# A hybrid decoder layer on one core: transposes of x and of the second norm inside projection columns, RWKV's turned keys in 2 KB runs, decayed keys of the right-hand sides turned by VectorE

## The chip, the cores and the metric

One core of one Trainium2 chip. The metric is the device time of one execution in microseconds (us), given as the median of several runs.

## The reference, cut to what matters

The input x is 1 x 2048 x 1024, in float32, as everything is. The layer runs two kinds of linear recurrence side by side, then a feed-forward block.

```python
h = _rmsnorm(x, norm1_w[l])
proj = h @ w_in[l]                                   # 3840 columns
...
o_hg = _hgrn2_mixer(...)                             # 4 heads of 128: columns q, f, i, g
o_rw = _rwkv7_mixer(...)                             # 8 heads of 64: r, k, v and three low-rank inputs
x = x + jnp.concatenate([o_hg, o_rw], axis=-1) @ w_out[l]
x = x + _conv_ffn(_rmsnorm(x, norm2_w[l]), ...)      # width 2816, causal convolution of 3
...
return _rmsnorm(x, final_norm_w)
```

RWKV's recurrence for each head, with a 64 x 64 state S, is

```python
sa = jnp.einsum('bhvk,bhk->bhv', S, at)
S = S * wt[:, :, None, :] + sa[..., None] * bt[:, :, None, :] + vt[..., None] * kt[:, :, None, :]
y = jnp.einsum('bhvk,bhk->bhv', S, rt)
```

The kernel computes it in chunks of 64 tokens: within a chunk, the vectors `sa` of all tokens solve a triangular system, whose matrix is made of products of decayed keys. Its right-hand sides hold, for each token, the decayed key `at` (what the state adds is a product with it) and what the values of the chunk's earlier tokens add.

## The kernel before, in words

**Phase 1** (to about 1250 us) does norm, projection, both recurrences and the out-projection of the first three blocks of tokens; the rest is the last block's out-projection and the feed-forward block, which the change leaves as they are. Phase 1 takes the 2048 tokens in 4 blocks of 512. Channels lie on the 128 partitions and tokens along the free axis.

`dense()` yields TensorE's large work as a list of jobs per block. The main one is a *column* ("P"): 128 columns of `w_in` times the normed x of the block, hh + hl (high and low part), over 8 slices k of 128 channels, three products of 128 x 512 each (`mm3`, L270 to L272), so 24 wide matmuls into one bank of PSUM. Two banks called `pj` are used in turn. The column's eviction (`ev_rkv`, `ev_q` and so on) reads the bank on ScalarE, and for most kinds on VectorE too, and only then the bank is free for the column after the next. A block has 31 columns in this order: 1 low-rank, 6 rkv, 8 of HGRN2 (q, f, v, g for two heads), 1 low-rank, 6 rkv, 8 of HGRN2. Every ScalarE operation goes through the helper `act` (L122) and every split in high and low part through L247 to L255, so these lines stand for many operations in the profile.

Other jobs are inserted between columns by their place in the list (`extra`, L543 on):
- "E" runs `load4` (four DMAs of 128 rows of the next block's x into `xt`) or `norm4` (scales each row by its norm, in place).
- "T" runs `turn` (L437): 8 groups, each of four 128 x 128 transposes on TensorE (L443) into a `pj` bank, which ScalarE copies back into `xt`. The next block's x is so turned in one go, for blocks 1, 2 and 3.
- "N" runs `transposed` (L258) for the second norm of block nb - 2: the rows come back from DRAM (`x1d`), are turned in the same manner (L264), scaled by ScalarE (`to_h2`, L490) and stored to DRAM (`h2d`) by a DMA of the SP queue (L494). It runs twice in phase 1's columns.
- "O" is the out-projection of block nb - 2.

RWKV's heads are worked in 8 *supers* (`rw_super`): one block of tokens and two pairs of heads (index u) each. HGRN2's heads are 16 units (`hg_unit`). The main loop takes one piece of each stream in turn and then as many dense pieces as a fixed credit holds, so pieces of the heads lie among the columns in the instruction queues. Engines take their queue strictly in order, and DMAs that a stream issues with `dma` stand in SP's queue in the order of the program.

A super, as far as the change touches it: VectorE makes the decayed keys `AT` (inside the tile `AR`) and `KB`. TensorE makes the products `M` (L730), VectorE masks them (L733). The triangular blocks go through DRAM into `E` (L745, L748), and VectorE inverts 32 x 32 blocks in 31 steps (L802, L804). Its result is transposed by VectorE into `TZ` (L808) and `TTs` (L814), and TensorE goes on with it at L821, L834 and L847. Meanwhile two things are turned from channels on partitions to tokens on partitions:
- `KBT`, the turned keys: VectorE transposes 32 x 32 squares of `KB` into `KBb` (L754), and 16 DMAs on SP move the squares to their partitions (L757), in runs of 128 bytes. TensorE reads `KBT` at L867 as weights (64 channels of one chunk and head per matmul, neighbours in memory) and in half of L881 as moving data.
- `RHS`, the right-hand sides: TensorE transposes `AT` (8 transposes per super, L765) into PSUM and two ScalarE copies (L774, L775, seen as L122) put it in `RHS`. The other half of `RHS` comes from L782 on. L847 reads it.

Of the kernel before, what the change touches and what calls it, by code (L numbers as in the profile page):

```python
# [67 lines left out]
def tile_layer(ctx, tc, consts, x, norm1_w, w_in, hg_lb_logits, hg_norm_w, rw_shift_mu, rw_w0, rw_w2,  # L68
# [205 lines left out]
    def phase1(c1):  # L274
# [162 lines left out]
        def turn(nb):  # L437

            t_ = rows[nb]
            for k in range(KD):  # L440
                tp = bank("pj")
                for i in range(4):
                    TE.transpose(tp[:, i * P:(i + 1) * P], t_[:, i, k * P:(k + 1) * P], ident)  # L443
                act(t_[:, :, k * P:(k + 1) * P], tp.rearrange("p (i t) -> p i t", i=4), AF.Copy)
                yield 436
# [43 lines left out]

        def to_h2(nb):  # L490
            def evict(k, tp, w):
                t_ = wp.tile([P, BLK], F32, tag="wraw", name="h2", bufs=4)
                act(t_, tp, AF.Copy, scale=w)
                dma(h2d[nb][k * P:(k + 1) * P, :], t_)  # L494
            return evict
# [20 lines left out]
        def dense():  # L516
# [63 lines left out]
            ahead = iter(())  # L580
            for n, jb in enumerate(jobs):
# [8 lines left out]
                if jb[0] == "T":  # L590
                    yield from turn(jb[1])
                    continue
                if jb[0] == "N":
                    yield from transposed(four_tiles(rows.pop(jb)), "n2", lambda: bank("pj"), to_h2(jb[1]))
                    continue
# [51 lines left out]
        def rw_super(nb, s_):  # L647
# [102 lines left out]
            KBT = tile_("KBT", [2, 8, P], "KBT")  # L750
            KBb = tile_("UV", [16, 4, 32], "KBb")
            KBv = KBb.rearrange("p n a c -> p (n a) c")
            for u in U:
                V.transpose(KBv[:, 32 * u:32 * u + 32], KB[:, 4 * u:4 * u + 4].rearrange("p b k (a t) -> p (b k a) t", t=32))  # L754
            for g in range(4):
                for a in range(4):
                    dma(KBT[32 * a:32 * a + 32].rearrange("p u i t -> p (u i) t")[:, :, 32 * g:32 * g + 32],  # L757
                        KBb[32 * g:32 * g + 32, :, a, :])
# [3 lines left out]
            tp = bank2()  # L762
            for u in U:
                for b in range(4):
                    TE.transpose(tp[:, u, b * P:(b + 1) * P], AT[:, u, 2 * b:2 * b + 2, :], ident)  # L765
            tpv = tp.rearrange("p u (b h t) -> p (u b) h t", h=2, t=64)
# [7 lines left out]
            act(RHS[64:128, :, :, 0:64], tpv[0:64], AF.Copy)  # L774
            act(RHS[0:64, :, :, 0:64], tpv[64:128], AF.Copy)  # L775
# [87 lines left out]
            for u in U:  # L863
                for ch in range(8):
                    b, e = ch // 2, ch % 2
                    for h in range(2):
                        TE.matmul(xp[h * 64:h * 64 + 64, u, ch * 64:ch * 64 + 64], KBT[:, u, ch, h * 64:h * 64 + 64],  # L867
                                  UV[:, 4 * u + b, e, h * 64:h * 64 + 64], start=ch == 0, stop=False,
                                  tile_position=(0, h * 64), skip_group_check=True)
# [755 lines left out]
```

## Time and profile before

| | before |
|---|---|
| time, median of 3 runs | 2650.35 us (2645.74 to 2656.13) |
| profiled execution | 2645.42 us |
| its span | 2643.6 us |
| mean granted TensorE clock | 0.994 |
| DMA | 380298 packets, 518.98 MB, mean 196 GB/s |
| packets under 512 B | 114463 |

The span is what the profiler recorded from the first instruction to the last; the execution's own time is a little longer. In the views, "L443" is line 443 of the kernel before; "out<-in" are the tiles that an instruction writes and reads; in square brackets stands how long the engine waited ahead of the instruction, and for which engine, tile and line. A row of the waits reads: instruction that waited, what it waited for, then sum in us, number of waits and the longest. A row with a count (x512) gives shortest, middle and longest duration in ns and the first and last time in us. A row of windows gives length, then busy time of PE, PEld, DVE, ACT, POOL and SP with instruction counts, then granted clock, the DMA engines' busy share and GB/s.

### The profile page before, as it was taken

How to read it: one execution, taken by the hardware profiler on the slowest of the kernel's cores; microseconds unless marked ns; L12 is line 12 of the kernel's file. 1: busy time of each engine (PE TensorE's matmuls, PEld its weight loads, DVE VectorE, ACT ScalarE, POOL GpSimd, SP SyncE). 2: the span in 40 equal slices, each digit the busy share in tenths (PEclk: the TensorE clock that was granted, in tenths of full speed). 3: DMA queues.
4: the chain of work that ended last, by engine and by line, in shares of the span. 5: the costliest groups of instructions: out<-in, count | busy, mean ns of one | idle time of the engine just before them, and what ended most of it. 6: DMA issues, size and time to landing. Idle time of an engine off the chain costs nothing.

```text
span 2643.6 us, 51054 instructions
## 1 busy us (share of the span) xinstructions
PE 2547.0 (96%) x19467; PEld 2046.8 (77%) x19467; DVE 1963.7 (74%) x3744; ACT 1372.7 (52%) x2258; POOL 382.1 (14%) x686
## 2 busy tenths in 40 slices
PE   7999999999999999899899999999999999999998
PEld 5877777777777767777678888887888887888887
DVE  4868677676576765777678789988988887766556
ACT  5555444555545555344466654556554544545444
POOL 6433222212222122232100000000000000000000
PEclk9999999999999999999999999999999999999999
DMA  8846463555655565845583467747763553998655
GB/s 304 239 147 195 152 168 116 143 159 205 190 173 138 174 212 179 261 151 150 181 287 124 136 221 257 240 154 232 245 203 129 171 171 128 334 321 283 200 191 187
DMA packets 380298, 518.98 MB, mean 196 GB/s; under 512 B 114463, under 2 KB 211093, under 8 KB 380053
## 3 DMA queue, kind: packets, MB, share of 16 engines
q1 hardware_dynamic: 325521, 337.38, 40.1%
q0 software_dynamic: 54464, 178.32, 20.9%
q8 instruction: 153, 2.51, 0.4%
q14 instruction: 92, 0.75, 0.1%
q10 hardware_dynamic: 68, 0.02, 0.0%
HBM read 372.99 MB, written 134.22 MB: 192 GB/s over the span
## 4 chain that ended last, share of the span: by engine, by line
PE 70%; DVE 11%; ACT 8%; DMA 7%; issue 3%; POOL 0%; SPq 0%; DVEq 0%; ACTq 0%; POOLq 0%
PE pj L270 7%; PE pj L271 7%; PE pj L272 6%; PE ua L270 5%; PE ua L272 5%; PE ua L271 5%; PE da L271 3%; PE da L272 3%; PE da L270 3%; PE ud L271 2%; PE ud L270 2%; PE ud L272 2%; PE db L272 2%; PE db L271 2%; PE db L270 2%
## 5 line engine op out<-in xcount | busy, mean ns | idle before, releaser
L270 PE MATMUL pj<-hh,wh 128*128 128x512 f32 x960 | 391.6, 408 | 6.1 <-ACT rkv L122 4.0
L271 PE MATMUL pj<-hl,wh 128*128 128x512 f32 x960 | 377.4, 393 | 0.0
L272 PE MATMUL pj<-hh,wl 128*128 128x512 f32 x960 | 377.4, 393 | 0.0
L270 PE MATMUL ua<-Bh,uwh 128*128 128x512 f32 x704 | 276.4, 393 | 3.5 <-ACT m L122 2.2
L272 PE MATMUL ua<-Bh,uwl 128*128 128x512 f32 x704 | 274.3, 390 | 0.0
L271 PE MATMUL ua<-Bl,uwh 128*128 128x512 f32 x704 | 274.1, 389 | 0.0
L270 PEld LDWEIGHTS pj<-hh,wh 128*128 128x128 f32 x960 | 180.9, 189 | 54.5 <-issue 7.0
L272 PEld LDWEIGHTS pj<-hh,wl 128*128 128x128 f32 x960 | 180.8, 188 | 39.4 <-DMA wl<-Win171l 0.3
L271 PEld LDWEIGHTS pj<-hl,wh 128*128 128x128 f32 x960 | 181.0, 189 | 35.0 <-DVE hl L488 0.5
L254 ACT CAST uwh<-uraw 128x512 fp32r<-128x512 f32 x220 | 134.3, 617 | 135.0 <-PE ua L271 55.7
L255 DVE TENSOR_TENSOR dal<-draw,dah 128x512 fp32r<-128x512 f32 x138 | 95.2, 690 | 108.3 <-ACT dah L254 105.7
L255 DVE TENSOR_TENSOR uwl<-uraw,uwh 128x512 fp32r<-128x512 f32 x220 | 147.1, 684 | 34.3 <-ACT uwh L254 34.3
L254 ACT CAST dah<-draw 128x512 fp32r<-128x512 f32 x138 | 85.8, 621 | 160.0 <-PE da L271 75.5
L270 PEld LDWEIGHTS ua<-Bh,uwh 128*128 128x128 f32 x704 | 132.2, 188 | 33.9 <-ACT m L122 5.6
L272 PEld LDWEIGHTS ua<-Bh,uwl 128*128 128x128 f32 x704 | 132.2, 188 | 28.1 <-DVE uwl L255 0.4
L271 PEld LDWEIGHTS ua<-Bl,uwh 128*128 128x128 f32 x704 | 132.3, 188 | 26.7
L270 PE MATMUL ud<-Bh,uwh 128*128 128x512 f32 x352 | 138.0, 392 | 0.0
L1495 POOL DMA_DIRECT2D gd<-y x2 | 1.1, 542 | 943.1 <-DVE y L1493 943.1
L272 PE MATMUL ud<-Bh,uwl 128*128 128x512 f32 x352 | 137.1, 390 | 0.0
L271 PE MATMUL ud<-Bl,uwh 128*128 128x512 f32 x352 | 137.0, 389 | 0.0
L271 PE MATMUL da<-dbl,dah 128*128 128x512 f32 x332 | 129.4, 390 | 0.2 <-DVE dbl L255 0.2
L272 PE MATMUL da<-dbh,dal 128*128 128x512 f32 x332 | 129.2, 389 | 0.0
(582 smaller groups left out, 6203.0 us busy)
## 6 DMA issues: line engine op xcount, KB each, us to landing
uraw<-in_w_up_dram SPq DMA_DIRECT2D x176, 256.0 KB, 3.2
woraw<-in_w_out_dram POOLq DMA_DIRECT2D x96, 256.0 KB, 3.6
br<-gd SPq DMA_DIRECT2D x88, 256.0 KB, 4.3
draw<-Sg SPq DMA_DIRECT2D x88, 256.0 KB, 3.0
draw<-Tw SPq DMA_DIRECT2D x88, 256.0 KB, 3.9
gd<-y SPq DMA_DIRECT2D x86, 256.0 KB, 3.0
Sg<-br SPq DMA_DIRECT2D x72, 256.0 KB, 2.2
xt<-x1d SPq DMA_DIRECT2D x32, 512.0 KB, 6.5
```

Source lines behind the costliest of these rows:

```text
L254: S.copy(hi, src)
L255: V.tensor_sub(lo, src, hi.bitcast(F32))
L270: TE.matmul(acc, lh, rh, start=first, stop=False, skip_group_check=skip)
L271: TE.matmul(acc, lh, rl, start=False, stop=False, skip_group_check=skip)
L272: TE.matmul(acc, ll, rh, start=False, stop=last, skip_group_check=skip)
L1495: (dma if end is None else nc.gpsimd.dma_start)(gd_[2 * h + b][fb * P:(fb + 1) * P, :], ys[0][:, b * BLK:(b + 1) * BLK])
```

## The change

Three edits, all in phase 1.

**Transposes inside columns.** `turn` now makes one group of four transposes, and `turn2` does so for the second norm. Both only queue the group in `turns`; a column takes one group from it after its slice k = 1 and one after k = 5. The eight groups of x are queued one per column, from 22 places after the block's start on, those of the second norm two per column from 8 places on. `load4` and `norm4` move a few places ahead. ScalarE's copies and the DMAs to `h2d` stay as many.

**Turned keys.** VectorE writes its squares of `KB` so that the 16 chunks n of one channel lie side by side: `KBb` is [4, 32, 16] instead of [16, 4, 32], and each of the 16 DMAs moves runs of 2 KB (512 floats) per partition instead of 16 runs of 128 bytes. `KBT` becomes [128 channels, 16], and the matmuls read the 64 channels of one chunk and head at a step of 16 floats.

**Right-hand sides.** VectorE transposes 32 x 32 squares of `AT` into a new tile `ATb`, and 16 DMAs per super, in runs of 128 bytes, place them in `RHS`. The transposes of TensorE with their PSUM tile and the two ScalarE copies go.

```diff
-        def turn(nb):
...
+        def turn(nb, k):
+            def f():
+                t_ = rows[nb]
                 tp = bank("pj")
                 for i in range(4):
                     TE.transpose(tp[:, i * P:(i + 1) * P], t_[:, i, k * P:(k + 1) * P], ident)
                 act(t_[:, :, k * P:(k + 1) * P], tp.rearrange("p (i t) -> p i t", i=4), AF.Copy)
-                yield 436
+            return f
+        def turn2(key, k):
+            def f():
...
+                h2 = wp.tile([P, BLK], F32, tag="wraw", name="h2", bufs=4)
+                act(h2, tp, AF.Copy, scale=vec("n2", k))
+                dma(h2d[key[1]][k * P:(k + 1) * P, :], h2)
+            return f
...
-                    extra += [(at[nb] + 18, ("E", load4(nb + 1, x[0], (nb + 1) * BLK))),
-                              (at[nb] + 22, ("E", norm4(nb + 1))), (at[nb] + 25, ("T", nb + 1))]
+                    extra += [(at[nb] + 17, ("E", load4(nb + 1, x[0], (nb + 1) * BLK))),
+                              (at[nb] + 20, ("E", norm4(nb + 1)))]
+                    extra += [(at[nb] + 22 + k, ("T", turn(nb + 1, k))) for k in range(KD)]
                 if nb >= 2:
-                    extra += [(at[nb] + 6, ("E", load4(("N", nb - 2), x1d[nb - 2], 0))),
-                              (at[nb] + 10, ("E", norm4(("N", nb - 2)))), (at[nb] + 11, ("N", nb - 2))]
+                    extra += [(at[nb] + 4, ("E", load4(("N", nb - 2), x1d[nb - 2], 0))),
+                              (at[nb] + 7, ("E", norm4(("N", nb - 2))))]
+                    extra += [(at[nb] + 8 + k // 2, ("T", turn2(("N", nb - 2), k))) for k in range(KD)]
...
+                    if k in (1, 5) and turns:
+                        turns.pop(0)()
...
-            KBT = tile_("KBT", [2, 8, P], "KBT")
-            KBb = tile_("UV", [16, 4, 32], "KBb")
-            KBv = KBb.rearrange("p n a c -> p (n a) c")
-            for u in U:
-                V.transpose(KBv[:, 32 * u:32 * u + 32], KB[:, 4 * u:4 * u + 4].rearrange("p b k (a t) -> p (b k a) t", t=32))
+            KBT = tile_("KBT", [P, 16], "KBT")
+            KBb = tile_("UV", [4, 32, 16], "KBb")
+            for u in U:
+                V.transpose(KBb[:, :, :, 8 * u:8 * u + 8].rearrange("p a c n -> p n a c"),
+                            KB[:, 4 * u:4 * u + 4].rearrange("p b k (a t) -> p (b k) a t", t=32))
             for g in range(4):
                 for a in range(4):
-                    dma(KBT[32 * a:32 * a + 32].rearrange("p u i t -> p (u i) t")[:, :, 32 * g:32 * g + 32],
-                        KBb[32 * g:32 * g + 32, :, a, :])
+                    dma(KBT[32 * a:32 * a + 32, 32 * g:32 * g + 32].rearrange("p c n -> p (c n)"),
+                        KBb[32 * g:32 * g + 32, a].rearrange("p c n -> p (c n)"))
+
+            def keys(rs, n, h):
+                return KBT[rs, h * 64:h * 64 + 64, n]
...
-            tp = bank2()
-            for u in U:
-                for b in range(4):
-                    TE.transpose(tp[:, u, b * P:(b + 1) * P], AT[:, u, 2 * b:2 * b + 2, :], ident)
-            tpv = tp.rearrange("p u (b h t) -> p (u b) h t", h=2, t=64)
+            ATb = tile_("XH", [8, 2, 2, 32], "ATb")
+            ATv = ATb.rearrange("p n e a c -> p (n e a) c")
+            for u in U:
+                V.transpose(ATv[:, 16 * u:16 * u + 16], AT[:, u].rearrange("p c (a t) -> p (c a) t", t=32))
+            for g in range(4):
+                for e in range(2):
+                    for a in range(2):
+                        r0, c0 = er0(e) + 32 * a, 32 * (g % 2)
+                        dma(RHS[r0:r0 + 32, :, g // 2, c0:c0 + 32], ATb[32 * g:32 * g + 32, :, e, a, :])
...
-            act(RHS[64:128, :, :, 0:64], tpv[0:64], AF.Copy)
-            act(RHS[0:64, :, :, 0:64], tpv[64:128], AF.Copy)
...
-                        TE.matmul(xp[h * 64:h * 64 + 64, u, ch * 64:ch * 64 + 64], KBT[:, u, ch, h * 64:h * 64 + 64],
+                        TE.matmul(xp[h * 64:h * 64 + 64, u, ch * 64:ch * 64 + 64], keys(slice(0, P), 8 * u + ch, h),
...
-                                       else KBT[rs_, u, 2 * b + e, h * 64:h * 64 + 64])
+                                       else keys(rs_, 8 * u + 2 * b + e, h))
```

In the instruction queues this looks as follows; the rows of the changed kernel carry its own line numbers. First, TensorE's queue before, at the first block of x that is turned, between two columns. `xt` holds the rows of x; L1083 and L1084 are pieces of an HGRN2 head.

```order
L270 MATMUL pj<-hh,wh 128x512
L271 MATMUL pj<-hl,wh 128x512
L272 MATMUL pj<-hh,wl 128x512
L443 MATMUL pj<-ident,xt 128x128 x8
L1083 MATMUL rw<-part,group 128x512
L443 MATMUL pj<-ident,xt 128x128 x10
L1084 MATMUL rw<-part,group 128x512
L1083 MATMUL rw<-part,group 128x512
L1084 MATMUL rw<-part,group 128x512
L443 MATMUL pj<-ident,xt 128x128 x14
L270 MATMUL pj<-hh,wh 128x512
```

The same queue now, at one of the eight groups of that block; the six wide matmuls are the slices k = 0 and 1 of a column.

```order
L1096 MATMUL hg<-part,ones 128x512
L270 MATMUL pj<-hh,wh 128x512
L271 MATMUL pj<-hl,wh 128x512
L272 MATMUL pj<-hh,wl 128x512
L270 MATMUL pj<-hh,wh 128x512
L271 MATMUL pj<-hl,wh 128x512
L272 MATMUL pj<-hh,wl 128x512
L443 MATMUL pj<-ident,xt 128x128 x4
L270 MATMUL pj<-hh,wh 128x512
```

Thirty-two transposes in a row, with four pieces of the heads among them, became groups of four that stand apart, each with a column's matmuls on both sides. Of the 40 groups in the program 23 stand right behind six wide matmuls of their column, 8 behind eighteen, and 9 behind some number between, since pieces of the heads lie elsewhere.

Second, TensorE's queue before in the first super, where `AT` is turned; L770 turns the values, whose tile is named by its buffer.

```order
L270 MATMUL pj<-hh,wh 128x512
L271 MATMUL pj<-hl,wh 128x512
L272 MATMUL pj<-hh,wl 128x512
L765 MATMUL rw<-ident,AR 128x128 x8
L770 MATMUL rw<-cst,rkv_681 128x128 x8
L270 MATMUL pj<-hh,wh 128x512
```

And the same place now, where L784 is the former L770.

```order
L270 MATMUL pj<-hh,wh 128x512
L271 MATMUL pj<-hl,wh 128x512
L272 MATMUL pj<-hh,wl 128x512
L784 MATMUL rw<-cst,rkv_681 128x128 x8
L270 MATMUL pj<-hh,wh 128x512
```

The eight transposes are gone; nothing else stands between.

Third, SP's queue before in the fifth super, which falls together with the second norm's stores to `h2d`.

```order
L757 DMA KBT<-KBb 32x16x32
L494 DMA h2d_151<-h_8360 128x512
L494 DMA h2d_151<-h_8390 128x512
L745 DMA Ed<-M 32x16x32 x4
L757 DMA KBT<-KBb 32x16x32 x2
L748 DMA E<-Ed 64x1024 x2
L757 DMA KBT<-KBb 32x16x32 x11
L424 DMA xt<-in_x_dram 128x1024 x4
```

And now, where L456 is the store to `h2d`, L764 the keys, L752 and L755 the two moves of `E`, and L780 the right-hand sides.

```order
L764 DMA KBT<-KBb 32x512 x5
L752 DMA Ed<-M 32x16x32 x4
L764 DMA KBT<-KBb 32x512
L780 DMA RHS<-ATb 32x8x32 x2
L755 DMA E<-Ed 64x1024 x2
L780 DMA RHS<-ATb 32x8x32 x14
L424 DMA xt<-in_x_dram 128x1024 x4
```

All keys but one now stand ahead of `Ed`; between `Ed` and `E` stand one DMA of the keys and two of the right-hand sides, and the other 14 follow `E`, ahead of the loads of x for the next block.

On VectorE two transposes of `KB` into `KBb` stand where they stood, and two of `AT` into `ATb` follow among the masks of `M`. The whole program has on each engine, before and now: TensorE 14621 and 14557 instructions, VectorE 3746 and 3762, ScalarE 2217 and 2201, GpSimd 690 and 690, SP 1353 and 1481.

More of the change, by code (lines that the diff above doesn't have):

```diff
@@ L435, in four_tiles @@
             return [t_[:, i, :] for i in range(4)]
-        def turn(nb):
-            t_ = rows[nb]
-            for k in range(KD):
+        def turn(nb, k):
+            def f():
+                t_ = rows[nb]
                 tp = bank("pj")
@@ L444, in turn @@
                 act(t_[:, :, k * P:(k + 1) * P], tp.rearrange("p (i t) -> p i t", i=4), AF.Copy)
-                yield 436
+            return f
+        def turn2(key, k):
+            def f():
+                t_ = rows[key]
+                tp = bank("pj")
+                for i in range(4):
+                    TE.transpose(tp[:, i * P:(i + 1) * P], t_[:, i, k * P:(k + 1) * P], ident)
+                h2 = wp.tile([P, BLK], F32, tag="wraw", name="h2", bufs=4)
+                act(h2, tp, AF.Copy, scale=vec("n2", k))
+                dma(h2d[key[1]][k * P:(k + 1) * P, :], h2)
+            return f
         def split_h(nb, k):
@@ L488, in to_h @@
             V.scalar_tensor_tensor(hl[:, k, :], tp, w, hh[:, k, :].bitcast(F32), ALU.mult, ALU.subtract)
[L490 to L495, printed above, removed]
         def constants():
@@ L580, in dense @@
             ahead = iter(())
+            turns = []
             for n, jb in enumerate(jobs):
@@ L590, in dense @@
                 if jb[0] == "T":
[L591 to L594, printed above, removed]
+                    turns.append(jb[1])
                     continue
```

## The prediction

> **What bounds the kernel now.** I read the page first (busy shares, then the chain that ended last), then the waits of TensorE in the first 1250 us, where all the edited code runs, and last the timeline around each edited step.
>
> ```profile
> span 2643.6 us, 51054 instructions
> PE 2547.0 (96%) x19467; PEld 2046.8 (77%) x19467; DVE 1963.7 (74%) x3744; ACT 1372.7 (52%) x2258; POOL 382.1 (14%) x686
> PE 70%; DVE 11%; ACT 8%; DMA 7%; issue 3%; POOL 0%; SPq 0%; DVEq 0%; ACTq 0%; POOLq 0%
> ```
>
> TensorE is busy for 96% of the span and holds 70% of the chain. It takes its instructions in order, so what an edit is worth is read off as TensorE time: instructions that leave or join its queue, and gaps in it. The work of the other engines counts only where TensorE waits for it.
>
> ```profile
> PE rw L867 <- ACT M L122: 9.7, 6, 3.6
> PE pj L443 <- ACT hf L122: 4.1, 2, 2.1
> PE rw L821 <- DVE TZ L808: 3.8, 4, 1.4
> ```
>
> These are sums of waits (us, times, longest). L443 is the transposes of x that the change moves. It waits for hf, a column of the projection whose bank ScalarE has not emptied, and, in the timeline below, for xt, its own evictions. The first of the three blocks of these transposes looks like this on TensorE (start, length, work):
>
> ```profile
> 212.16 0.39 PE L270 MATMUL pj<-hh,wh 128*128 128x512 f32 x1
> ...
> 216.01 0.39 PE L272 MATMUL pj<-hh,wl 128*128 128x512 f32 x1
> 216.25 0.60 PE L443 MATMUL pj<-ident,xt 128*128 128x128 f32 x4
> 218.82 0.66 PE L443 MATMUL pj<-ident,xt 128*128 128x128 f32 x4 [1.98 <-ACT hf L122]
> ...
> 221.75 0.44 PE L443 MATMUL pj<-ident,xt 128*128 128x128 f32 x2 [0.35 <-ACT xt L122]
> ...
> 225.22 0.50 PE L270 MATMUL pj<-hh,wh 128*128 128x512 f32 x1 [0.20 <-ACT xt L122]
> ...
> 243.21 1.03 PE L765 MATMUL rw<-ident,AR 128*128 128x128 f32 x8
> ...
> L765 PE MATMUL rw<-ident,AR x64: 270/272/300, 98.4 to 1199.3; 128*128 128x128 f32 x64
> ```
>
> From 212.16 to 216.01 lie 17 wide matmuls, 0.227 us each: the projection runs with no gap. Eight transposes back to back take 1.03 us, of which the last is 0.27 long (272 ns, the middle one of all 64), so one costs (1.03 - 0.27) / 7 = 0.109. Between 216.24 and 225.22 TensorE does 32 transposes and 4 wide matmuls, 3.5 + 0.9 = 4.4 us, in 8.98.
>
> **The moved transposes.** The five places where whole blocks are turned, three for x and two for the second norm:
>
> ```profile
> 216.24:225.22 8.98, 5.93 (x37) 4.04 (x35) 8.98 (x11) 7.97 (x14) 3.62 (x6) 1.00 0.45 151
> 494.87:504.02 9.15, 6.73 (x37) 5.16 (x36) 9.15 (x12) 8.18 (x14) 1.07 (x2) 0.81 0.21 75
> 699.67:710.95 11.28, 9.68 (x102) 7.69 (x100) 11.21 (x21) 5.97 (x11) 1.27 (x2) 1.00 0.68 220
> 832.08:839.94 7.86, 5.93 (x40) 4.33 (x38) 7.86 (x9) 6.64 (x11) 1.07 (x2) 1.00 0.29 94
> 1034.48:1045.04 10.56, 9.29 (x102) 7.66 (x100) 10.49 (x19) 5.91 (x11) 1.26 (x2) 1.00 0.75 240
> ...
> 702.21 2.06 PE L730 MATMUL rw<-AR,KB 64*128 64x128 f32 x32
> ...
> 705.59 0.49 PE L730 MATMUL rw<-AR,KB 64*128 64x128 f32 x4 [0.52 <-DVE M L733]
> ...
> 834.26 0.50 PE L1084 MATMUL rw<-part,group 128*128 128x512 f32 x1 [1.35 <-DVE part L248]
> ```
>
> They last 47.8 us together. The three for x hold 4.4 us of instructions each, 13.2. The two for the second norm hold 32 transposes (3.5), four more of the same form (0.4) and two groups of L730 (2.06 each): 8.0 each, 16.0. What is left is 47.8 - 29.2 = 18.6 us of gaps. (In the second window the granted clock was 0.81, so part of its share is slower work.) Some 2.7 us of it wait for something else that stays: 1.35 and 0.52 in the rows above, two like the latter in the other window. I take **15.8 us as the gaps that go**.
>
> What is late next: in a column the transposes take the one bank that the column isn't filling, so the column before must have left it. This is an eviction of the costliest kind (rkv):
>
> ```profile
> 467.55 0.39 PE L272 MATMUL pj<-hh,wl 128*128 128x512 f32 x1
> 467.97 0.69 ACT L122 ACTIVATE rkv<-pj,omu 128x512 f32<-128x512 f32 x1 [1.21 <-PE pj L272]
> 468.69 0.75 DVE L313 SCALAR_TENSOR_TENSOR rkv<-pj,vt,rkv 128x511 f32<-128x511 f32 x1 [3.31 <-ACT rkv L122]
> ...
> 469.69 0.15 DVE L315 COPY lastc<-pj 128x1 f32<-128x1 f32 x1
> ...
> L122 ACT ACTIVATE sgm<-pj 128x512 f32<-128x512 f32 x32 | 19.1, 597 | 63.0 <-PE pj L272 62.8
> L346 DVE SCALAR_TENSOR_TENSOR hq<-pj,sgm 128x512 f32<-128x512 f32 x16 | 11.0, 686 | 45.2 <-ACT sgm L122 45.2
> ```
>
> The column's last matmul starts at 467.55, the bank is free at 469.84, 2.3 us later. By the order, 23 of the 40 groups stand right behind six matmuls of the next column, 7 x 0.227 = 1.6 us later, 8 behind eighteen, the others between. So such a column makes them wait 0.7, where nothing else lies between. A q or g column is free after 0.42 + 0.60 + 0.69 = 1.7 us (last two rows) and makes them wait 0.1; an f or v column needs ScalarE alone, and nothing waits. The columns ahead of the eight groups of x are rkv, rkv, q, f, v, g, q, f: 2 x 0.7 + 3 x 0.1 = 1.7 us a block; for the second norm rkv, q, f, v: 0.8. That is 3 x 1.7 + 2 x 0.8 = **6.7 us of new gaps**. Work of the heads that lies between takes from it, an engine that is behind adds to it (up to 1.98, as for hf); the ends are 0 and 15.8, as much as went. A group amid wide matmuls may cost a little more than 4 x 0.109; I put 0.6 us for all 40. The copies, square roots and DMAs that go with them are the same in number.
>
> **The right-hand sides.** Their 64 transposes leave TensorE, and two ScalarE copies for each of the eight pairs of heads leave ScalarE:
>
> ```profile
> L122 ACT ACTIVATE RHS<-rw 64x1024 f32<-64x1024 f32 x16 | 16.3, 1019 | 16.9 <-PE rw L765 16.8
> ```
>
> 64 x 0.109 = **7.0 us** less for TensorE, on its path. ScalarE has 16.3 us less to do, and 16.8 less in which it stood waiting for these transposes; TensorE gains from that only where it waits for ScalarE. I count 0 and keep -5 as the end. VectorE gets 16 transposes of 512 elements, and the SP queue 128 more DMAs. The nearest VectorE rows:
>
> ```profile
> L814 DVE STREAM_TRANSPOSE TTs<-TZ x32: 699/702/708, 138.8 to 1243.2; 32x512 f32<-32x512 f32 x32
> L808 DVE STREAM_TRANSPOSE TZ<-Ti x8: 1034/1044/1075, 137.4 to 1239.6; 128x512 f32<-128x512 f32 x8
> ```
>
> At 0.70 each that is 11.2 us, 1.4 for each pair of heads. It is hidden: between the transposes of KB and the first step of the triangular inverse VectorE has idle time in each of the eight cases, first and sixth here (length, busy):
>
> ```profile
> 86.00:108.70 22.70, 15.83 (x31) 1.00 1.00 256
> 839.60:865.60 26.00, 12.46 (x25) 1.00 0.81 174
> E<-Ed SPq DMA_DIRECT2D x16, 256.0 KB, 4.6
> KBT<-KBb SPq DMA_DIRECT2D x128, 64.0 KB, 4.5
> L757 SPq DMA_DIRECT2D KBT<-KBb x128: 591/640/2658, 89.3 to 1205.6; - x128
> ```
>
> 6.9 and 13.5 us idle. If that cover were gone, the 1.4 us would come late at L821, where TensorE waits for TZ already: 11 us in all. On SP a DMA of KBT holds the queue for 0.64, so 16 more hold it for 10 us per pair. E, the one transfer that is wanted soon, stands behind at most two of them. The right-hand sides are read only after the inverse, whose first step comes 22.7 us after the keys' transposes in the first row. I count 0 for both.
>
> **The turned keys.** Longer runs make the transfers cheaper, which nothing waits for. But the keys now lie so that neighbours along a head are 16 floats (64 bytes) apart, and TensorE reads 64 of them per matmul, as weights at L867 and as moving data in half of L881:
>
> ```profile
> 1252.08 2.37 PE L867 MATMUL rw<-UV,KBT 128*64 128x64 f32 x64
> ...
> 1254.89 0.65 PE L881 MATMUL rw<-KBT,M 64*64 64x64 f32 x32
> ```
>
> Per pair of heads that is 2.37 + 2 x 0.65 = 3.7 us, 29 us in all. No row shows TensorE reading at such a step. VectorE does in L808 (each element 64 bytes from the last, 1044 ns), while L814 reads runs of two floats and needs 702 for as many: 1.49 times. Lower end: TensorE's reads are no slower, 0. Upper end: each element costs what it costs in L808, 1044 / 512 = 2.04 ns. Then 64 weight loads of 64 elements take 8.4 us in place of 2.37, and 64 moving reads, two at a time in separate halves of the partitions, 4.2 in place of 1.3: 8.9 x 8 = +71 us. I take the ratio, 0.49 x 3.7 x 8 = **+14.4 us**, because a ratio between two rows of the same size carries over better than a time of another engine. Written at that step, KBb may also take VectorE 0.7 us longer for 1024 elements, 11 us in all, within the idle time above.
>
> The Trainium skill ("SBUF — State Buffer", section "Door 1: The DMA port swizzle") states that SBUF is read in lines of 16 bytes, that full bandwidth needs two hits or more in a line, and that each step to a new line costs. L808 with one hit and L814 with two agree. By that rule the keys are slow for TensorE too, which is the case taken here or the rival below; the page gives no price for TensorE.
>
> **Sum**, against the profiled execution (2645.4 us, of which 2643.6 are span): -15.8 + 6.7 + 0.6 - 7.0 + 14.4 = -1.1, so 2644.3. The median of the three runs shown, 2650.35, lies 4.9 above that execution; a median of the changed kernel should lie as far above, at **2649**.
>
> **The rivals.** A measurement of this kernel can tell about 0.5%, 13 us, from no change.
>
> The keys cost in full (slower). One mechanism: every strided element takes 2.04 ns at L867 and L881, +71 in place of +14.4. That gives 2700.9, and 2705.8 as a median. For it: the measured VectorE row at the very same step, and that L867 reads 64 elements per weight load in so little time that any limit on lines shows. Against it: TensorE's reads in the moving matmuls run at 0.227 us for 512 floats, far above VectorE's rate, so its port need not share VectorE's limit. The kernel gets slower by over 13 us once the strided matmuls cost more than 29 us extra, that is once they take twice what they take now. The Trainium skill's line rule, read strictly, is this rival.
>
> The keys cost nothing (faster). -15.5, so 2629.9, as a median 2634.8, 0.58% faster.
>
> ```profile
> L821 PE MATMUL rw<-TZ,M x512: 186/191/213, 138.5 to 1241.3; 32*32 32x32 f32 x171
> L834 PE MATMUL rw<-TTs,ZT x512: 191/191/258, 140.7 to 1243.7; 32*32 32x32 f32 x171
> ```
>
> For it: L821 reads TZ in runs of two floats at a step of 128 bytes and is as long as L834, which reads rows without gaps; against it, two floats are not one.
>
> The waits only move. The transposes wait in the columns for late evictions as long in sum as they did in blocks: 15.8 in place of 6.7, so +8.0, 2653.4, as a median 2658. For it: the hf wait of 1.98, and more small groups that each need a bank; against it, a column leaves 1.6 us before the bank is wanted and a block leaves none.
>
> That the change doesn't do what it says is ruled out by the order, where L765 is gone and the groups stand alone.
>
> **How the numbers follow.** Forecast 0.43 (chance inside it of over 13 us faster 0.22, of over 13 us slower 0.05), keys free 0.30 (0.75 faster), keys in full 0.15 (all slower), waits move 0.12 (0.15 slower). Faster 0.09 + 0.23 = 0.32; slower 0.02 + 0.15 + 0.02 = 0.19; within 0.5% 0.49. The range goes from 2623, keys free with the gaps wholly gone and 5 us for ScalarE (2634.8 - 6.7 - 5), to 2685, where the keys cost 50 of their 71 (2650.35 - 15.5 + 50).
>
> **What would show it.** Right: L867 near 3.5 us for 64 records and the KBT half of L881 near 1.0; 20 or so short gaps before L443 and L453, under 0.7 each; no row of L765's kind; unchanged times from 1300 us on. Wrong: L867 at 2.4, or at 8; waits of L847 for RHS or of the inverse for E, which would mean that the SP queue is too slow; longer waits of L821 for TZ, which would mean that VectorE's idle time did not cover its new work.

## The result, and the profile after

The changed kernel takes 2685.53 us (median of 4 runs, 2683.98 to 2687.98) against 2650.07 for the kernel before (4 runs): ratio 1.0133, 95% interval 1.0116 to 1.0150. It is 35 us slower, half a microsecond outside the range; 2649 with 0.49 on "no change" was forecast. The profiled execution took 2683.98 us. Its page, after:

```profile
span 2682.2 us, 51060 instructions
PE 2571.8 (96%) x19403; PEld 2065.5 (77%) x19403; DVE 1986.1 (74%) x3760; ACT 1357.9 (51%) x2242; POOL 381.9 (14%) x686
PE 49%; DVE 10%; DMA 7%; issue 5%; ACT 3%; SPq 1%; POOL 1%; DVEq 0%; POOLq 0%; ACTq 0%
```

TensorE is as full as before, with 64 instructions fewer and 24.8 us more busy time. The chain's shares sum to 76% here and to 99% before, so that its 49% for TensorE can't be set against the 70%; I read what follows from groups, waits and timelines. The keys of the last pair of heads, in TensorE's timeline after (the former L867 and L881):

```profile
1280.75 3.82 PE L879 MATMUL rw<-UV,KBT 128*64 128x64 f32 x64
...
1285.02 1.11 PE L893 MATMUL rw<-KBT,M 64*64 64x64 f32 x32
```

3.82 us where 2.37 stood, and 1.11 where 0.65 stood. The time from each instruction's start to the next one's, summed over both lines and all eight pairs and without waits, grows from 38.4 to 55.9 us, 17.5 more. (With its waits the sum before is 40.3; the 15.6 us that an expectation below names is the difference to that.) Next, TensorE's waits after, those ahead of the moved transposes and one, for UV, that was 0.3 us before:

```profile
PE pj L443 <- DVE hgg L370: 5.3, 2, 3.2
PE rw L794 <- ACT UV L122: 4.1, 5, 1.9
...
PE pj L443 <- DVE hq L346: 3.1, 4, 1.4
```

The longest of them in TensorE's timeline (in brackets the wait and its cause):

```profile
237.98 0.39 PE L271 MATMUL pj<-hl,wh 128*128 128x512 f32 x1
241.53 1.12 PE L443 MATMUL pj<-ident,xt 128*128 128x128 f32 x4 [3.16 <-DVE hgg L370]
...
242.87 0.63 PE L270 MATMUL pj<-hh,wh 128*128 128x512 f32 x1
243.29 0.63 PE L271 MATMUL pj<-hl,wh 128*128 128x512 f32 x1
```

VectorE's timeline at the same time:

```profile
231.08 3.70 DVE L760 STREAM_TRANSPOSE KBb<-KB 128x1024 f32<-128x1024 f32 x2
...
235.55 0.70 DVE L775 STREAM_TRANSPOSE ATb<-AR 128x512 f32<-128x512 f32 x1
236.18 0.38 DVE L986 TENSOR_TENSOR hf<-hf 128x256 f32<-128x256 f32 x1
236.48 0.69 DVE L775 STREAM_TRANSPOSE ATb<-AR 128x512 f32<-128x512 f32 x1
...
240.73 0.74 DVE L370 SCALAR_TENSOR_TENSOR hgg<-pj,vt,sgm 128x512 f32<-128x512 f32 x1
```

And the window around it, whose third number from the end is the granted clock, the share of full speed at which TensorE was allowed to run:

```profile
238.00:244.00 6.00, 2.84 (x10) 2.19 (x9) 5.66 (x13) 1.14 (x2) 1.29 (x2) 0.74 0.76 215
```

VectorE works from 231 on without a pause, the new transposes among it, and empties the column's bank only at 241.47. Behind the stop the wide matmuls start 0.42 us apart instead of 0.227, and the window grants 0.74 of the clock. The forecast summed stops, but no slow stretch behind one. Over the runs the median granted clock is 0.992 before and 0.987 after; 0.005 of 2685 is 13 us, an estimate that overlaps with the stops.

### The profile page after: what moved, and what is told of

Read it like the earlier page. It is cut to its first block, busy times and chain, and to the rows that moved or that the text cites. A ratio compares the mean times of both kernels' runs of the same rounds, so it can differ in the third digit from the quotient of the medians.

```text
span 2682.2 us, 51060 instructions
## 1 busy us (share of the span) xinstructions
PE 2571.8 (96%) x19403; PEld 2065.5 (77%) x19403; DVE 1986.1 (74%) x3760; ACT 1357.9 (51%) x2242; POOL 381.9 (14%) x686
## 4 chain that ended last, share of the span: by engine, by line
PE 49%; DVE 10%; DMA 7%; issue 5%; ACT 3%; SPq 1%; POOL 1%; DVEq 0%; POOLq 0%; ACTq 0%
PE ua L270 4%; PE ua L272 4%; PE ua L271 4%; PE pj L270 3%; PE pj L271 3%; PE pj L272 3%; PE da L271 3%; PE da L272 3%; PE da L270 3%; PE ud L271 2%; PE ud L272 2%; PE ud L270 2%; PE db L270 2%; PE db L271 2%; PE db L272 2%
## 5 line engine op out<-in xcount | busy, mean ns | idle before, releaser
L270 PE MATMUL pj<-hh,wh 128*128 128x512 f32 x960 | 397.0, 414 | 2.4 <-DVE xh L413 2.2
L272 PE MATMUL pj<-hh,wl 128*128 128x512 f32 x960 | 380.2, 396 | 0.0
L270 PE MATMUL ua<-Bh,uwh 128*128 128x512 f32 x704 | 276.8, 393 | 4.8 <-ACT m L122 4.1
L272 PE MATMUL ua<-Bh,uwl 128*128 128x512 f32 x704 | 274.5, 390 | 0.0
L270 PEld LDWEIGHTS pj<-hh,wh 128*128 128x128 f32 x960 | 182.6, 190 | 52.4 <-issue 10.3
L272 PEld LDWEIGHTS pj<-hh,wl 128*128 128x128 f32 x960 | 182.2, 190 | 40.6 <-issue 1.2
L270 PEld LDWEIGHTS ua<-Bh,uwh 128*128 128x128 f32 x704 | 132.3, 188 | 35.6 <-ACT m L122 7.7
L272 PEld LDWEIGHTS ua<-Bh,uwl 128*128 128x128 f32 x704 | 132.2, 188 | 28.6 <-DVE uwl L255 0.8
L270 PE MATMUL ud<-Bh,uwh 128*128 128x512 f32 x352 | 138.0, 392 | 0.0
L272 PE MATMUL ud<-Bh,uwl 128*128 128x512 f32 x352 | 137.1, 389 | 0.0
L272 PE MATMUL da<-dbh,dal 128*128 128x512 f32 x332 | 129.2, 389 | 0.0
```

Of the source, the lines that this page charges most:

```text
L270: TE.matmul(acc, lh, rh, start=first, stop=False, skip_group_check=skip)
L272: TE.matmul(acc, ll, rh, start=False, stop=last, skip_group_check=skip)
```

## The experiments

Each was timed against the kernel before on the same chip; ratios are to it, with 95% intervals. The medians of that kernel lie between 2648.4 and 2650.1 us in these sessions.

**The three edits apart.** Nothing but the parts of the diff: turns, keys, right-hand sides, and turns with right-hand sides.

Turns alone. 

> The changed kernel with the keys and the right-hand sides as before: only the transposes inside columns. Theory A (VectorE's queue is the cause: 2.8 us more of its work per super stand ahead of column evictions, the bank comes late, TensorE stops and its clock is halved for 3.4 us or more): without that work the gaps ahead of the groups shrink below the 11 us seen with all three edits and the clock is as before; about 10 us faster than before, 2635 to 2645. Rival B (groups inside columns make TensorE wait by themselves): as many gaps as with all edits, half-clock stretches too; 5 to 15 us slower than before.

Measured: 2654.4, ratio 1.0025 (1.0011 to 1.0038), 6 us slower.

Keys alone. 

> Only the turned keys in 2 KB runs, read at a step of 16 floats. Both theories: the two groups of matmuls take 15.6 us more in all, as in the changed kernel. Theory A adds VectorE's 11.5 us, which come through in part as waits and half-clock stretches: 20 to 30 us slower than before. Rival B: 15 to 17 us slower and no new waits.

Measured: 2675.0, ratio 1.0098 (1.0077 to 1.0118), 26.5 us slower: theory A's range.

Right-hand sides alone. 

> Only the right-hand sides turned by VectorE. TensorE does 64 transposes less, 7 us. Theory A: VectorE's 11 us and the later landing of E take back as much or more, -3 to +8 us. Rival B: -7 us, or a little more.

Measured: 2647.9, ratio 1.0001 (0.9987 to 1.0015): nothing gained, as theory A has it, where rival B has 7 us.

Turns and right-hand sides. 

> Transposes inside columns and right-hand sides by VectorE, keys as before. Theory A: the turns' gain of about 10 us and the right-hand sides' near nothing: 5 to 15 us faster than before, unless the 1.4 us per super on VectorE ahead of the evictions bring the stops back, then about the same. Rival B: 0 to 8 us slower. If the parts add up, this run plus the keys alone gives the 35 us of the whole change.

Measured: 2665.3, ratio 1.0062 (1.0044 to 1.0081), 16.8 us slower, 11 more than the two apart, with a median clock of 0.986. Both forecasts missed, and the parts don't add up: this and the keys alone make 43 us, the whole change 35.

So theory A fell for the turns: without any new work on VectorE they lose, where 8.5 us of gain were forecast. Rival B has the time, but not the gaps, fewer here than with all edits: 7.1 us in sum against 11 (start of a group to the start before it, beyond the usual 0.23). The forecast was 6.7, and the loss was elsewhere.

**The step of the keys.** Two layouts between: runs of 32 channels times S chunks, neighbours S floats apart (the diff has S for the 4 and 2 of the two runs).

```diff
-            KBT = tile_("KBT", [P, 16], "KBT")
+            KBT = tile_("KBT", [16 // S, P, S], "KBT")
...
+            def keys(rs, n, h):
+                return KBT[rs, n // S, h * 64:h * 64 + 64, n % S]
```

S = 4. 

> Only the turned keys, in a layout between: runs of 512 bytes, neighbours of a head 4 floats (16 bytes) apart. Theory C (TensorE pays once neighbours are 16 bytes or more apart, however far): the two groups of matmuls are as long as at a step of 16 floats, about 3.5 us at the weights and 1.0 at each half; VectorE's transposes too, 0.7 us more each; 20 to 27 us slower than before. Rival D (the price grows with the distance): between, 8 to 15 us slower.

S = 2. 

> The same with a step of 2 floats (8 bytes) and runs of 256 bytes; VectorE's transposes come in 16 pieces of 128 elements a partition per super in place of 2 of 1024. Theory C: two floats in 16 bytes, TensorE's matmuls as long as before; the time within 5 us of before, the small pieces on VectorE included. Rival E (every step other than 1 costs): 10 to 20 us slower.

(VectorE's pieces at S = 2 are 8 of 256 elements per super.) Measured: S = 4 2669.8, ratio 1.0078 (1.0060 to 1.0096); S = 2 2642.8, ratio 0.9976 (0.9965 to 0.9987), 6.9 us faster than before, a little more than the 5 us within which theory C put it; what made it faster was not looked for. TensorE's timeline at the last pair of heads, first with S = 16 (keys alone):

```profile
1280.30 4.03 PE L870 MATMUL rw<-UV,KBT 128*64 128x64 f32 x64 [0.19 <-ACT M L122]
...
1284.77 1.08 PE L884 MATMUL rw<-KBT,M 64*64 64x64 f32 x32
```

The same with S = 4:

```profile
1272.37 4.34 PE L870 MATMUL rw<-UV,KBT 128*64 128x64 f32 x64 [0.17 <-ACT M L122]
...
1277.15 1.10 PE L884 MATMUL rw<-KBT,M 64*64 64x64 f32 x32
```

And with S = 2:

```profile
1245.45 2.52 PE L870 MATMUL rw<-UV,KBT 128*64 128x64 f32 x64 [0.17 <-ACT M L122]
...
1248.43 0.65 PE L884 MATMUL rw<-KBT,M 64*64 64x64 f32 x32
```

Theory C holds: 8 bytes cost TensorE next to nothing, 16 bytes cost all, 64 no more. The Trainium skill ("SBUF — State Buffer", "Door 1: The DMA port swizzle") says that full bandwidth needs two hits in a 16-byte line, and these three rows agree, for weights and for moving data. Its next sentence, that 4 fp32 can be strided free, they do not bear out: a step of 4 floats already paid in full.

Of the 26.5 us of the keys 18.9 are TensorE's reading, by the same sums as above (12.3 at the weights, 6.6 at the halves). Some waits grew as well. TensorE's in the run with the keys alone:

```profile
PE rw L730 <- DVE M L733: 5.4, 3, 1.8
...
PE rw L785 <- ACT UV L122: 4.4, 4, 2.6
```

VectorE's, ahead of the first step of the inverse:

```profile
DVE etmp L805 <- DMA E<-Ed: 19.1, 5, 6.8
```

And ScalarE's:

```profile
ACT UV L122 <- DMA KBT<-KBb: 11.8, 5, 6.1
```

Before, the first two stood at 1.6 and 0.3, the others at 0. On SP 11 to 16 of the 16 moves of the keys now stand ahead of E, in the first four supers, where 6 to 10 stood; with S = 2 it is 5 to 10, and neither of the last two waits is there. UV's copy goes to the tile that `KBb` had, so ScalarE must wait for the keys' moves.

Yet these waits are not what is left of the 26.5 us. Up to the start of the last head product (`gdt`), first before, then with the keys alone, the window's length and TensorE's busy time are:

```profile
0.00:1306.20 1306.20, 1226.38 (x13640) 961.63 (x13641) 900.91 (x2140) 658.45 (x1107) 365.73 (x656) 0.99 0.59 182
0.00:1334.80 1334.80, 1256.30 (x13640) 985.42 (x13641) 911.80 (x2139) 658.85 (x1106) 364.25 (x656) 0.98 0.55 178
```

TensorE is idle for 79.8 us and for 78.5: what some waits gained others lost (the wait for M ahead of the keys as weights fell from 9.7 us to 3.6). It is busy 29.9 us longer, 11 more than the reading. The granted clock stands at half for 44.4 us of the window, against 27.3 before; half of the difference, 8.5 us, is an estimate of that loss. With S = 4 VectorE and ScalarE wait in the same two places, 11.8 and 8.4 us, but the clock is at half for 27.3 us only; that run is 20.2 us slower, and its reading 20.9 longer. So beyond the reading the keys cost clock, as far as one execution of each shows; what set the clock back there was not traced further.

**VectorE's longer transposes.** Half of each transpose is done twice, to the same end:

```diff
+                V.transpose(KBv[:, 32 * u:32 * u + 16], KB[:, 4 * u:4 * u + 2].rearrange("p b k (a t) -> p (b k a) t", t=32))
```

> The kernel before with half of each transpose of the keys done twice on VectorE, to the same end: 16 more instructions of about 0.6 to 0.7 us, at the place where the step of 16 floats costs 0.7. Theory F (VectorE's queue delays column evictions and the masks of M, so that its time comes through): 5 to 11 us slower than before. Rival G (idle time hides it, as the prediction put it): within 3 us of before; then all of the 26 us of the keys is TensorE's reading, 15 to 17 us, and what follows from it.

Measured: 2651.6, ratio 1.0006 (0.9994 to 1.0018). Rival G: VectorE's idle time does hide as many microseconds as the step costs it.

**Another slot.** `if k == 4 and turns:` in place of `k in (1, 5)`, turns only.

> Only the transposes inside columns, one group per column after slice 4 in place of slices 1 and 5, so that the column before has had 3.4 us to leave its bank. Theory H (the waits for the bank, 7 us, and the half-clock stretches behind them are what the turns cost): no such waits, 8 to 14 us faster than with slices 1 and 5, 2640 to 2646. Rival I (the gaps move to the heads' waits, since the bursts were time in which VectorE and ScalarE caught up): the waits ahead of the groups go all the same, but the time stays within 4 us of the turns at slices 1 and 5, 2650 to 2658.

Measured: 2656.4, ratio 1.0029 (1.0017 to 1.0042). The gaps ahead of the groups shrank to 1.2 us in sum and the time stayed: rival I. The gaps ahead of the groups were not what the turns cost.

**The credit.** `turn` yielded 436 for each group, which the main loop took from its dense credit; in the new form a group takes none. One line gives it back, in the turns alone; in the other run the kernel before, with its whole blocks, yields 0 for each group.

```diff
                     if k in (1, 5) and turns:
                         turns.pop(0)()
+                        yield 436
```

Turns with credit. 

> Only the transposes inside columns (after slices 1 and 5), but each group takes 436 ns of the main loop's credit, as the groups of the kernel before did, so that the heads' pieces keep their place among the columns. Theory J (what the turns cost is that the heads' pieces come later among the columns, 17 us of dense work in sum): back by 6 us or more, 2640 to 2649. Rival K (the gaps move to the heads' waits whatever the pace): as the turns alone, 2651 to 2658.

Whole blocks without credit. 

> The kernel before with its transposes in whole blocks, but taking none of the main loop's credit; nothing else changes. Theory J: it alone costs what the turns cost, 4 to 9 us slower than before. Rival K: within 3 us of before.

Measured: with credit 2639.0, ratio 0.9962 (0.9950 to 0.9975), 9.9 us faster than before and 15.4 faster than the turns without it; whole blocks without credit 2676.2, ratio 1.0100 (1.0080 to 1.0119), 27.3 us slower. Both go theory J's way, the first a little beyond its range and the second far beyond its 4 to 9 us. In that second run's profile TensorE is idle 8.5 us longer than before up to the last head product, and the clock is at half for 61.4 us against 27.3; why whole blocks pay so much more for the lost credit than the groups do stays open. What moves is seen by counting the wide matmuls (L270 to L272 into `pj`, 24 to a column) that start before the last product of each super, the one with `gdt`:

```
columns ahead of it, supers 1 to 8
before               22.0  36.8  52.2  66.6  89.5  104.2  127.5  143.0
turns with credit    22.0  36.8  52.1  66.5  89.4  104.2  127.5  143.0
turns alone          22.0  37.5  52.9  68.0  90.4  105.4  128.1  143.2
the whole change     22.0  37.5  52.9  68.0  90.4  105.4  128.1  143.2
```

From the first group on, the heads' pieces come 0.2 to 1.4 columns later (with whole blocks and no credit too, by 0.2 to 1.4). One place where that costs is the end of the out-projection of the second block of tokens. TensorE's timeline there, turns alone:

```profile
966.97 0.73 PE L270 MATMUL pj<-wh,hh 128*128 128x512 f32 x2 [2.50 <-ACT wh L254]
...
971.90 0.79 PE L270 MATMUL pj<-hh,wh 128*128 128x512 f32 x1 [2.41 <-DVE xh L413]
```

ScalarE's, turns alone:

```profile
962.51 1.28 ACT L118 ACT_TABLE_LOAD   x1
963.81 0.81 ACT L122 ACTIVATE yo<-yo,vt 128x512 f32<-128x512 f32 x1
964.64 1.63 ACT L122 ACTIVATE yo<-yo,lnx 64x512 f32<-64x512 f32 x2
966.29 0.62 ACT L254 CAST wh<-woraw 128x512 fp32r<-128x512 f32 x1
```

TensorE's at the same end, turns with credit:

```profile
955.54 0.73 PE L270 MATMUL pj<-wh,hh 128*128 128x512 f32 x2 [0.91 <-ACT wh L254]
...
966.93 0.51 PE L270 MATMUL pj<-hh,wh 128*128 128x512 f32 x1 [0.58 <-DVE xh L413]
```

ScalarE's, turns with credit:

```profile
952.63 1.64 ACT L122 ACTIVATE yo<-yo,lnx 64x512 f32<-64x512 f32 x2
954.88 0.61 ACT L254 CAST wh<-woraw 128x512 fp32r<-128x512 f32 x1
```

Without credit the last pieces of a super (`yo`) stand in ScalarE's queue ahead of the last weights of `w_out`, and TensorE waits 2.50 and 2.41 us; with credit they are done at 954.27, some 12 us before that end, where they hold up an earlier weight for 0.91 us; the last weights come without a wait, and 0.58 is left at the end.

**Repairs put together.** Step 2 with the right-hand sides; the whole change with step 2; then, with credit: step 2 without the right-hand sides, the whole change, the whole change with step 2; and the turns with twice the credit (872).

Step 2 and right-hand sides. 

> The turned keys at a step of 2 floats, and the right-hand sides turned by VectorE; transposes in whole blocks as before. If the two edits add up: 6 to 7 us faster than before, about 2643, the same as the keys at a step of 2 floats alone. Rival (TensorE's 7 us come through once the keys' waits are gone): 10 to 14 us faster, 2636 to 2640.

Measured: 2651.8, ratio 1.0014 (1.0001 to 1.0027). Neither: the right-hand sides cost 9 us beside the step of 2.

The whole change at step 2. 

> The whole change with the keys at a step of 2 floats in place of 16. If the keys' cost is the step alone: 32 us faster than the change (26 that the keys cost, 6 that they gain), 2650 to 2656. If the step costs less beside the other two edits than alone: the turns and right-hand sides by themselves less 6 us, 2657 to 2661.

Measured: 2664.4, ratio 1.0058 (1.0041 to 1.0075). Neither: 21 us faster than the change, 3 slower than the dearer forecast.

Credit and step 2. 

> The transposes inside columns with 436 ns of credit each, and the keys at a step of 2 floats; right-hand sides as before. If the two gains add up (10 and 6 us): 16 us faster than before, about 2633. If they take away the same waits: 10 us faster, about 2639.

Measured: 2639.4, ratio 0.9960 (0.9947 to 0.9973). They do not add up.

The whole change with credit. 

> The whole change with one line more, the credit of 436 ns for each group. Theory J (the heads' pieces moved among the columns cost 16 us in the change too): 16 to 17 us faster than the change, 2667 to 2671. If the other two edits move the pieces anyway: under 8 us faster, over 2677.

Measured: 2663.6, ratio 1.0060 (1.0039 to 1.0081), 22 us faster than the change, a little more than theory J.

The whole change with credit and step 2. 

> All three edits with both repairs (credit, and a step of 2 floats). If each repair holds in full: as the credit and the step without the right-hand sides, 2630 to 2636. If the right-hand sides cost 9 us beside the step of 2, as they did with transposes in whole blocks: 2640 to 2645.

Measured: 2647.0, ratio 0.9995 (0.9982 to 1.0008), beyond both forecasts, 8 us more than without the right-hand sides.

Turns with twice the credit. 

> Only the transposes inside columns, with 872 ns of credit for each group, twice what they take: the heads' pieces come earlier among the columns by as much as they came later without credit. Theory L (only heads that come later cost): within 4 us of the run with 436 ns, 2635 to 2643. Rival M (the order before is a tuned alignment, and any move costs): 5 us or more slower than with 436 ns, over 2644.

Measured: 2642.1, ratio 0.9976 (0.9964 to 0.9988). Theory L. By the same count the heads come 0.1 to 0.7 columns earlier than before. The median is 3 us above that with a credit of 436, which the intervals don't tell from nothing; coming later cost 15.

**VectorE's part in the right-hand sides.** Credit and step 2, with VectorE's two transposes of `AT` per super added, which nothing reads.

```diff
+            for u in U:
+                V.transpose(ATv[:, 16 * u:16 * u + 16], AT[:, u].rearrange("p c (a t) -> p (c a) t", t=32))
```

> Credit and a step of 2 floats, with VectorE's transposes of the decayed keys added (0.7 us each, two per super) and nothing taken away: their result isn't read, and the right-hand sides come from TensorE and ScalarE as before. Theory N (VectorE's 11 us are what the third edit costs): 8 us or more slower than credit and step 2 alone, 2646 to 2655. Rival O (the transfers on SP and the later arrival cost it): within 4 us of them, 2636 to 2643.

Measured: 2641.1, ratio 0.9965 (0.9954 to 0.9977). Rival O: VectorE's time by itself is not it. (TensorE's transposes still stand there; that VectorE's time counts only once they are gone is not excluded.) Whether SP's queue, the moves themselves or the later arrival is, was not told apart; in the profiles of step 2 with the right-hand sides, with credit and without, no engine waits for E or for the moves into `RHS`.

## Why the prediction was wrong, step by step

The measured medians lead from before to the change in five steps, each one edit (in another order the steps would differ: the keys at a step of 16 cost 26.5 us alone):

```
before                                  2648.9
+ turns, with credit                    2639.0    -9.9
+ keys at a step of 2                   2639.4    +0.4
+ right-hand sides by VectorE           2647.0    +7.6
+ step of 16 instead of 2               2663.6   +16.6
+ credit taken away (the change)        2685.5   +21.9
```

Set against the terms of the sum, the credit is off by 21.9 us, the right-hand sides by 14.6 (+7.6 for -7.0), the keys by 2.6 (+17.0 for +14.4), the turns by -1.4 (-9.9 for -8.5). TensorE's window up to the last head product of the changed kernel shows where the time went:

```profile
0.00:1335.60 1335.60, 1247.93 (x13582) 978.52 (x13583) 925.43 (x2158) 643.26 (x1091) 366.12 (x657) 0.98 0.58 181
```

Against the same window before, TensorE is idle 7.9 us more and busy 21.6 more: 17.5 for reading the keys, 6.9 less without the transposes of `AT`, and 11.0 that go with the clock, at half for 51.2 us here and 27.3 before (half of the difference, 12.0, is an estimate). The sum had no term for the clock.

**The moved transposes**, "15.8 us as the gaps that go" and 6.7 of new ones: their sum came out. -15.8 + 6.7 + 0.6 = -8.5; with credit it is -9.9, and the new gaps there sum to 5.9 us. The 6.7 was partly luck: some 20 gaps under 0.7 us were forecast, the longest behind rkv columns; the turns alone have 10, up to 2.1, with credit 10, up to 1.1, and none of them waits for an rkv column (they wait for hq, hgg, hf and h, where they name a cause). The step failed in what it left out. `turn` issued, besides transposes, copies and DMAs, a yield of 436; the diff shows it go, and I gave it no price. Without it the heads' pieces moved by up to 1.4 columns, which cost 15 us with the turns alone and 22 in the whole change. This is the step that turned the forecast over: the heads' place among the columns was taken as fixed. The rival "the waits only move" had nearly the right time for the turns (+8.0 against +6), but not the place: the waits ahead of the groups were short, and taking them away (slot 4) gained nothing.

**The turned keys**, +14.4: TensorE's reading came to 17.5 us in the change and 18.9 alone, so the term was 3.1 to 4.5 us too small; that TensorE pays, and about how much, was right. The ratio of two VectorE rows, 1.49, stood for 1.61 at the weights and 1.71 at the halves. "The keys cost nothing" and "the keys cost in full" (8.4 us for 64 weight loads) both fell; VectorE's row carried over as a ratio, not as a time.

**"E stands behind at most two of them"** counted only the moves of the right-hand sides. The order showed that the keys' own moves had gone ahead of `Ed`, and that was not priced: VectorE waits for E for 15.4 us in the change and 19.1 with the keys alone, a sign of being wrong that the prediction had named, and ScalarE in the latter 11.8 us for the keys' moves, for which nothing was to wait. That these waits cost time is not shown: with the keys alone TensorE is idle no longer than before, and the 7.6 us beyond its reading, which the prediction had at 0, go with the clock as far as one profile shows. VectorE's own 0.7 us per transpose were as forecast (1.94 for 1.22 us) and hidden, as the run with doubled work shows.

**The right-hand sides**, -7.0: TensorE's 6.9 us did go, but alone nothing was gained, and beside the other edits they cost 8 to 9 us. So the step "7.0 us less for TensorE, on its path" failed, with "I count 0 for both" behind it; that VectorE's added time alone costs nothing was right, and what takes the gain back stays open.

**"Unchanged times from 1300 us on"** did not hold in this profile. All head products with `gdt`, with the first and last start, before:

```profile
L936 PE MATMUL rw<-gdt,g x32: 590/592/592, 198.9 to 1306.2; 128*128 128x512 f32 x32
```

And after:

```profile
L948 PE MATMUL rw<-gdt,g x32: 590/592/697, 199.7 to 1335.6; 128*128 128x512 f32 x32
```

From the last one to the end of the span it is 1337.4 us before and 1346.6 after, though no line there was edited. Turns alone have 1346.1, turns with credit 1337.4, so 8.7 of the 15 us between these two profiles lie there; whole blocks without credit have 1340.4. Part of it is the heads' late end. TensorE's timeline after, at the start of the last block's out-projection:

```profile
1342.52 0.50 PE L1282 MATMUL wacc<-woh,Bh 128*128 128x512 f32 x1 [2.15 <-ACT Bh L247]
1344.44 0.77 PE L1282 MATMUL wacc<-woh,Bh 128*128 128x512 f32 x1 [1.42 <-DVE yo L950]
```

It waits for what the last heads hand over. All six profiled kernels without the credit wait so, 1.7 to 2.2 and then 1.4 us, and have the clock at half for 3.4 or 6.8 us right behind; the thirteen others have neither. That is worth some 3 us, an estimate (about 1 us more of waits than the others have within 20 us of that point, and half of 3.4). The rest stays open: over all nineteen profiles, one execution of each, this part takes from 1337.4 to 1346.6 us.

## What to carry to other kernels

Count what a moved piece tells the scheduler as one of its instructions: if it paid for its time in a hand-made interleaving, it must go on paying, or everything behind it shifts. Before longer runs for a DMA are bought with a step in memory, ask who reads at that step; an intermediate layout with two neighbours kept together was 6.9 us faster by itself, with half the packets for these moves, where the full one cost 26 us. Here the turns with their credit (2639.0 us) beat both kernels, and neither the keys nor the right-hand sides added to that.

## What the runs showed of the hardware

TensorE reads fp32 weights and moving data at a step of 8 bytes about as fast as without gaps (2.52 and 0.65 us at the last pair, against 2.37 and 0.65; 38.6 against 38.4 over all pairs), and at 16 bytes as slowly as at 64 or more so (4.34 against 4.03 for the weights). VectorE's transposes into `KBb`, for as many elements, grow too (count times middle duration): 19.6 us in all before, 25.9 at 8 bytes in pieces of 256, 34.6 at 16 bytes in pieces of 512, 30.9 at 64 bytes. The first two, before and at 8 bytes (shortest, middle and longest in ns):

```profile
L754 DVE STREAM_TRANSPOSE KBb<-KB x16: 1192/1224/1243, 85.7 to 1184.9; 128x1024 f32<-128x1024 f32 x16
```

```profile
L754 DVE STREAM_TRANSPOSE KBb<-KB x64: 399/404/448, 84.1 to 1183.3; 128x256 f32<-128x256 f32 x64
```

A stop of TensorE of 3.16 us was followed by wide matmuls at half pace (0.42 us apart) until 244.15. The Trainium skill ("TensorE: Matmul & The Clock Gate", "Part 1: The HAM clock gate") has the clock halved after an idle window of about 3.4 us; here shorter stops were enough: this one, and in the turns alone that of 2.50 us with one of 0.49 behind it, where the window from 969.2 to 975.9 grants 0.50 of the clock, from before the stop of 2.41 that follows. In all nineteen profiles the clock is either full or half, and the stretches at half, away from a profile's start and end, last 3.41 us or a multiple of it.
